# Layer 1's mixing of a two-layer diffusion block: the first map's tiles in pairs, by seven products of 256 tokens

## The chip, the cores and the metric

The kernel runs on one core of a Trainium2 chip. The core has a matrix engine (TensorE, PE in the rows; its weight loads are PEld), three elementwise engines (VectorE or DVE, ScalarE or ACT, GpSimd or POOL) and a queue that issues transfers (SyncE, SP). The metric is the device time of one execution in microseconds, the median over the runs shown.

## The reference, cut to what matters

Two layers over 512 tokens of width 1024. Every layer ends in a squared-ReLU mixing:

```
def _sq_relu_mlp(h, w1, w2):
    return jnp.square(jax.nn.relu(h @ w1)) @ w2
h_lat = h_lat + mod_l[5] * _sq_relu_mlp(
    _modulate(_rmsnorm(h_lat, norm2_g[i]), mod_l[3], mod_l[4]), mlp_w1[i], mlp_w2[i])
```

`w1` is 1024 x 4096 and `w2` is 4096 x 1024, all in float32. The change is in `h @ w1` of layer 1; after that layer only the final norm is left.

## The kernel before, in words

Everything lies with channels on the 128 partitions and the 512 tokens along a row. A float32 product is made of three products of two-part numbers: an operand is split into a high part (a cast on ACT) and a low part (the difference, on DVE or POOL), and PE adds high x high, high x low and low x high into one buffer of PSUM (`split` L161, `proj_steps` L190). So a tile of 128 outputs with an inner size of 1024 is 8 x 3 = 24 matmuls with 512 tokens each.

`mlp` runs over four blocks of 1024 hidden channels. A block has eight f tiles (from `w1`, out of the normed activations `nh`, `nl`), each followed by `f_out`: ReLU and square on ACT, the square again and the low part `gl` on DVE. Then it has eight r tiles (from `w2`, out of `gh`, `gl`), each added into the residual `h` by `h_add` on DVE. In block 0 the first four f tiles are made in two halves of 256 tokens, as the norm of the second half comes later; in block 3 the last four r tiles are made in halves too, and the final norm hangs on them.

Weights come as tiles of 128 x 1024 floats. SP loads them into two rings of buffers `raw` (four and three, tile k goes to ring k mod 2); each is then split into `whi`, `wlo` (two buffers in a ring), the cast always on ACT, the low part on DVE or POOL by turns (`w_prep`). `w_next` asks for loads seven tiles ahead and splits two ahead. Each engine takes its instructions in the order in which the program writes them, and waits on semaphores of the others. `residual` and `residual_norm` make r tiles, `grow` makes a piece of the modulation on DVE (in layer 0's mixing, 48 pieces). PSUM gives six buffers `mm` of 512 floats for f and r tiles.

Of the kernel before, what the change touches and what calls it, by code (L numbers as in the profile page):

```python
# [93 lines left out]
def body(ctx: ExitStack, tc: tile.TileContext, I, out):  # L94
# [6 lines left out]
    def f32(ap):  # L101
        return ap.bitcast(F32)
# [86 lines left out]

    def proj_steps(ps, w, ah, al, t0=0, n=T):  # L190
        k = len(ah)
        for i in range(k):
            c = slice(i * P, (i + 1) * P)
            wh = w[0]
            pe.matmul(ps, wh[:, c], ah[i][:, t0 : t0 + n], start=(i == 0), stop=False)  # L195
            yield
            pe.matmul(ps, wh[:, c], al[i][:, t0 : t0 + n], start=False, stop=False)  # L197
            yield
        for i in range(k):
            wl = w[1]  # L200
            pe.matmul(ps, wl[:, i * P : (i + 1) * P], ah[i][:, t0 : t0 + n], start=False, stop=(i == k - 1))  # L201
            yield

    def proj(*a):
        for _ in proj_steps(*a):
            pass
# [1229 lines left out]

    gk = [0]

    def grow(n=1):
        for _ in range(n):  # L1440
            k = gk[0]
            if k == len(gq):
                return
            gk[0] += 1
            while len(gin) < k + 2:
# [137 lines left out]

    def mlp(layer, ah_, al_, nrm, i_norm, shift_in, last_norm, mod_next, load=None):
        gate = mods[:, layer, 5, :]
        for blk in range(4):
            gh, gl = [None] * 8, [None] * 8
# [15 lines left out]
            def pair(f, n, mids):  # L1603
# [398 lines left out]
```

## Time and profile before

| what | value |
| --- | --- |
| median of 3 runs (lowest, highest) | 1123.25 us (1123.15, 1125.39) |
| the profiled execution, its own time | 1122.43 us |
| its span from first to last instruction | 1120.6 us |
| mean granted TensorE clock | 0.989 |
| PE, DVE, ACT, POOL busy, share of the span | 97%, 62%, 39%, 37% |

The span is shorter than the execution's time by 1.8 us, which lie around it. Shares are means over stages of different kinds: layer 0's mixing with attention and long convolution is the first third, the two mixings by `mlp` are most of the rest. "Busy" of PE counts matmuls whose ends are modelled, so the pace is read from start to start of matmuls. What an engine waits for is in the lists of waits; idle time of an engine that nobody waits for costs nothing.

### The profile page before, as it was taken

The page shows a single profiled execution, that of the slowest core. Times are in us where ns is not written, and L with a number is a line of the kernel's source. Part 1 is how long each engine was busy: PE and PEld are TensorE (multiplying, and loading weights), DVE is VectorE, ACT ScalarE, POOL GpSimd, SP SyncE. Part 2 cuts the span into 40 slices and gives each one's busy share as a digit, 9 for nine tenths or more (in the row PEclk, how much of TensorE's full clock was granted, in tenths as well). Part 3 has the DMA queues.
Part 4 walks back from the last instruction along what each step waited for, and adds up shares of the span by engine and source line. Part 5 has one row for each costly group of instructions (what it writes and reads, how often), then busy time and mean ns, then how long its engine had stood idle before and what let it go on. Part 6 is the DMA issues. An engine that isn't in the chain of part 4 may idle for free.

```text
span 1120.6 us, 14729 instructions
## 1 busy us (share of the span) xinstructions
PE 1087.8 (97%) x5740; PEld 918.4 (82%) x5740; DVE 691.4 (62%) x1026; ACT 439.2 (39%) x740; POOL 412.4 (37%) x308
## 2 busy tenths in 40 slices
PE   8899999999999999999999999899999999999996
PEld 5488988788989988888888888898888888888886
DVE  6589899989856646686686674677333323322334
ACT  4455346666554531331242233375313312411431
POOL 4457337885654423122132123265211311231112
PEclk9899999999999999999999999999999999999998
DMA  9786754225432327457557553213322332231302
GB/s 339 273 270 213 255 172 138 71 69 170 150 134 76 114 94 245 168 199 242 198 189 241 187 173 132 76 39 113 113 75 75 113 113 75 76 126 62 113 1 75
DMA packets 48650, 161.36 MB, mean 144 GB/s; under 512 B 5250, under 2 KB 8578, under 8 KB 48452
## 3 DMA queue, kind: packets, MB, share of 16 engines
q1 hardware_dynamic: 46132, 149.93, 39.2%
q0 software_dynamic: 2448, 10.49, 2.7%
q8 instruction: 45, 0.74, 0.3%
q14 instruction: 25, 0.20, 0.1%
HBM read 156.20 MB, written 4.20 MB: 143 GB/s over the span
## 4 chain that ended last, share of the span: by engine, by line
PE 80%; DVE 11%; ACT 2%; DMA 2%; issue 2%; POOL 2%; SPq 0%; POOLq 0%; DVEq 0%; ACTq 0%
PE r L195 11%; PE r L197 11%; PE r L201 11%; PE f L201 10%; PE f L197 10%; PE f L195 10%; PE v L876 2%; DVE g L627 2%; PE u L195 1%; DVE nl L1509 1%; PE u L201 1%; PE u L197 1%; DMA g<-in_adaN 1%; PE f L1610 1%; DVE mx L1053 1%
## 5 line engine op out<-in xcount | busy, mean ns | idle before, releaser
L164 POOL TENSOR_TENSOR wlo<-raw,whi 128x1024 fp32r<-128x1024 f32 x77 | 194.6, 2531 | 518.1 <-ACT whi L163 384.7
L163 ACT CAST whi<-raw 128x1024 fp32r<-128x1024 f32 x135 | 139.8, 1042 | 174.5 <-PE r L197 153.9
L195 PE MATMUL r<-gh,whi 128*128 128x512 f32 (+1 forms) x576 | 207.3, 368 | 0.0
L197 PE MATMUL r<-gl,whi 128*128 128x512 f32 (+1 forms) x576 | 207.0, 368 | 0.0
L195 PE MATMUL f<-nh,whi 128*128 128x512 f32 (+1 forms) x512 | 191.4, 379 | 0.0
L197 PE MATMUL f<-nl,whi 128*128 128x512 f32 (+1 forms) x512 | 191.3, 378 | 0.0
L1522 DVE SCALAR_TENSOR_TENSOR h<-r,mods,h 128x512 f32<-128x512 f32 (+1 forms) x81 | 54.3, 671 | 170.0 <-PE r L201 169.8
L1600 DVE TENSOR_TENSOR r<-r 128x512 f32<-128x512 f32 (+1 forms) x72 | 53.8, 748 | 159.1 <-ACT gh L1599 159.0
L1598 ACT ACTIVATE r<-f 128x512 f32<-128x512 f32 (+1 forms) x72 | 39.5, 548 | 236.7 <-PE f L201 235.1
L201 PE MATMUL r<-gh,wlo 128*128 128x512 f32 (+1 forms) x576 | 130.2, 368 | 0.0
L195 PEld LDWEIGHTS r<-gh,whi 128*128 128x128 f32 x576 | 108.3, 188 | 19.2
L197 PEld LDWEIGHTS r<-gl,whi 128*128 128x128 f32 x576 | 108.4, 188 | 19.0
L201 PE MATMUL f<-nh,wlo 128*128 128x512 f32 (+1 forms) x512 | 121.3, 379 | 0.0
L201 PEld LDWEIGHTS r<-gh,wlo 128*128 128x128 f32 x576 | 100.5, 188 | 18.9
L195 PEld LDWEIGHTS f<-nh,whi 128*128 128x128 f32 x512 | 96.2, 188 | 19.0
L197 PEld LDWEIGHTS f<-nl,whi 128*128 128x128 f32 x512 | 96.3, 188 | 18.9
L201 PEld LDWEIGHTS f<-nh,wlo 128*128 128x128 f32 x512 | 92.3, 188 | 18.9
L1451 DVE CUSTOM_DVE_ANT_0 g<-g,sbcl 128x1024 f32<-128x1024 f32 x48 | 105.2, 2191 | 0.0
L164 DVE TENSOR_TENSOR wlo<-raw,whi 128x1024 fp32r<-128x1024 f32 x58 | 75.9, 1308 | 8.4 <-ACT whi L163 8.4
L195 PE MATMUL u<-ah,whi 128*128 128x512 f32 x160 | 63.3, 395 | 0.8 <-DVE v L882 0.8
L197 PE MATMUL u<-al,whi 128*128 128x512 f32 x160 | 62.5, 391 | 0.0
L723 POOL TENSOR_TENSOR wlo<-raw,whi 128x1024 fp32r<-128x1024 f32 x17 | 42.5, 2499 | 37.3 <-ACT whi L714 35.5
(374 smaller groups left out, 1874.3 us busy)
## 6 DMA issues: line engine op xcount, KB each, us to landing
raw<-in_w SPq DMA_DIRECT2D x128, 512.0 KB, 4.4
g<-in_adaT SPq DMA_DIRECT2D x80, 512.0 KB, 4.2
g<-in_adaN SPq DMA_DIRECT2D x16, 512.0 KB, 9.0
raw<-in_w_hy SPq DMA_DIRECT2D x12, 512.0 KB, 4.3
raw<-in_w_qk SPq DMA_DIRECT2D x8, 512.0 KB, 4.0
pth<-in_pth POOLq DMA_DIRECT2D x4, 768.0 KB, 6.3
raw<-in_w_out SPq DMA_DIRECT2D x5, 512.0 KB, 4.0
x<-in_xT SPq DMA_DIRECT2D x8, 256.0 KB, 6.4
```

What stands on the lines that cost most here:

```text
L163: act.copy(out=hi, in_=src)
L164: (lo_eng or dve).tensor_tensor(out=lo, in0=src, in1=f32(hi), op=ALU.subtract)
L195: pe.matmul(ps, wh[:, c], ah[i][:, t0 : t0 + n], start=(i == 0), stop=False)
L197: pe.matmul(ps, wh[:, c], al[i][:, t0 : t0 + n], start=False, stop=False)
L201: pe.matmul(ps, wl[:, i * P : (i + 1) * P], ah[i][:, t0 : t0 + n], start=False, stop=(i == k - 1))
L627: dve.tensor_tensor_reduce(out=g, in0=g, in1=sbc[0], scale=1.0, scalar=0.0, op0=ALU.mult, op1=ALU.add, accum_out=mods[:, 0, 2 + k // ND, k ...
L723: ew(pool if k else dve).tensor_tensor(out=wts[k][1], in0=raws[k], in1=f32(wts[k][0]), op=ALU.subtract)
L876: pe.matmul(pp[:, :256], a, b, start=(k == 0 and e == 0), stop=(k == ND - 1 and e == 2))
L1451: dve.tensor_tensor_reduce(out=gin[k], in0=gin[k], in1=sbc[0], scale=1.0, scalar=0.0, op0=ALU.mult, op1=ALU.add, accum_out=mods[:, layer, ...
L1522: dve.scalar_tensor_tensor(out=hs[d][:, seg], in0=pp[:, :n], scalar=gate[:, d : d + 1], in1=hs[d][:, seg], op0=ALU.mult, op1=ALU.add)
L1598: act.activation(out=r, in_=pp[:, :n], func=AF.Relu)
L1600: dve.tensor_tensor(out=r, in0=r, in1=r, op=ALU.mult)
```

## The change

In layer 1 the f tiles of blocks 1, 2 and 3 are made two at a time (`pair7`), twelve pairs. Two tiles are a product of weights cut in 2 x 2 (two tiles, two halves of the 1024 inputs) with activations cut in 2 x 2 (two halves of the inputs, two halves of the tokens); a form of Strassen's scheme makes it by seven products and not eight. A product is 4 x 3 matmuls of 256 tokens. The seven go in this order (buffer in PSUM, weights): `px` first half, W0; `py` first, W0; `py` second, W1; `pz` second, W2; `px` second, W3; `px` first, W1; `pz` first, W2. W0 is the first tile's weights, W1, W2 and W3 are or hold sums of both tiles' weights: POOL makes one sum into the scratch tile `scr` and one in place, DVE makes two into `scr` (`pair_sums`). The sums of the activations are made once, during block 0's r tiles (`act_sums`, into `th` and over the second half of `nh`, `nl`). The seven products are put together by five adds on DVE out of PSUM (into `s1`, `s2`, named r in the rows, and `u3`, named na) and a copy on ACT (`p1`). `finish` of a pair, six activations on ACT (ReLU, square, square again for each tile) and two low parts `gl` on DVE, is written into the next pair, behind its second and third product. `late=2` puts the last two of eight steps at the end of the r tile that follows the last pair.

```
...
+    def proj_steps(ps, w, ah, al, t0=0, n=T, late=0):
...
+        for part in (range(k - late), range(k - late, k)):
+            for i in part:
...
+    def w_split(k, src, eng, n=1024):
+        pl, tg, nr, nb, rp = streams["st"[k % 2]]
+        hi = pl.tile([P, 1024], F32R, name=nm("whi"), tag=tg + "whi", bufs=nb)
+        lo = pl.tile([P, 1024], F32R, name=nm("wlo"), tag=tg + "wlo", bufs=nb)
+        split(hi[:, :n], lo[:, :n], src, eng)
+        return hi, lo
+    def pair_sums(k):
+        if k in sums_done or k not in pairs:
+            return
+        sums_done.add(k)
+        a, b, t = wraw[k], wraw[k + 1], scr[0]
+        dve.tensor_tensor(out=t[:, :T], in0=b[:, :T], in1=a[:, :T], op=ALU.add)
+        dve.tensor_tensor(out=t[:, T : 2 * T], in0=t[:, :T], in1=a[:, T:], op=ALU.add)
     def w_prep(n):
         while len(wsp) < min(n, len(wsrc)):
             k = len(wsp)
-            eng = (dve, pool)[k // 2 % 2]
-            wsp.append(wload(None, pool if k in fast else eng, "st"[k % 2], wraw[k]))
+            if k in pairs:
+                a, b, t = wraw[k], wraw[k + 1], scr[0]
+                pool.tensor_tensor(out=t[:, 2 * T : 3 * T], in0=a[:, :T], in1=b[:, :T], op=ALU.add)
+                pool.tensor_tensor(out=b[:, :T], in0=b[:, :T], in1=b[:, T:], op=ALU.add)
+                wsp.append(w_split(k, a, pool))
+            elif k - 1 in pairs:
+                pair_sums(k - 1)
+                wsp.append(w_split(k, scr[0][:, : 2 * T], dve))
+            else:
+                eng = (dve, pool)[k // 2 % 2]
+                wsp.append(wload(None, pool if k in fast else eng, "st"[k % 2], wraw[k]))
...
+            th = ml.tile([P, 4, 2, 3, 256], F32R, name=nm("th"), tag="pth")
+            scr[0] = ml.tile([P, 2048], F32, name=nm("scr"), tag="ptl")
+            pairs.update(k0 + 16 * blk + f for blk in (1, 2, 3) for f in (0, 2, 4, 6))
+        def act_sums(i):
+            b1, b2, t = (ml.tile([P, T], F32, name=nm("b"), tag="sq", bufs=3) for _ in range(3))
+            x, y = slice(0, 256), slice(256, 512)
+            pool.tensor_tensor(out=b1, in0=f32(ah_[i]), in1=f32(al_[i]), op=ALU.add)
+            pool.tensor_tensor(out=b2, in0=f32(ah_[i + 4]), in1=f32(al_[i + 4]), op=ALU.add)
+            dve.tensor_tensor(out=t[:, x], in0=b1[:, x], in1=b1[:, y], op=ALU.subtract)
+            dve.tensor_tensor(out=t[:, y], in0=b2[:, y], in1=b1[:, y], op=ALU.subtract)
+            yield
+            dve.scalar_tensor_tensor(out=b1[:, y], in0=t[:, y], scalar=-1.0, in1=b1[:, x], op0=ALU.mult, op1=ALU.subtract)
+            dve.scalar_tensor_tensor(out=b2[:, y], in0=b1[:, y], scalar=-1.0, in1=b2[:, x], op0=ALU.mult, op1=ALU.subtract)
+            split(th[:, i, 0, 0:2, :], th[:, i, 1, 0:2, :], t.rearrange("p (a t) -> p a t", a=2), pool)
+            split(th[:, i, 0, 2, :], th[:, i, 1, 2, :], b1[:, y], pool)
+            split(ah_[i][:, y], al_[i][:, y], b2[:, y], pool)
+            yield
...
+        def product(o, w, c, b):
+            for i in range(4):
+                l = w[0][:, c + i * P : c + (i + 1) * P]
+                pe.matmul(o, l, b[i][0], start=(i == 0), stop=False)
+                pe.matmul(o, l, b[i][1], start=False, stop=False)
+            for i in range(4):
+                pe.matmul(o, w[1][:, c + i * P : c + (i + 1) * P], b[i][0], start=False, stop=(i == 3))
...
+            def pair7(f, before):
+                k = wk[0]
+                wk[0] += 2
+                w_fetch(k + 7)
+                w0, w1 = wsp[k], wsp[k + 1]
+                w2 = w_split(k, wraw[k + 1], dve)
+                x, y = slice(0, 256), slice(256, 512)
+                px, py, pz = ps_m("f"), ps_m("f"), ps_m("f")
+                small = [ml.tile([P, 256], F32, name=nm("na"), tag="na", bufs=4) for _ in range(2)]
+                p1, u3 = small
+                s1 = ml.tile([P, T], F32, name=nm("r"), tag="r", bufs=3)
+                twice = lambda v: v.rearrange("p (a t) -> p a t", a=1).to_broadcast([P, 2, 256])
+                both = lambda v: v.rearrange("p (a t) -> p a t", a=2)
+                product(px[:, x], w0, 0, b_part(0, 0))
+                act.copy(out=p1, in_=px[:, x])
+                product(py[:, x], w0, T, b_part(1, 0))
+                w3 = w_split(k + 1, scr[0][:, 2 * T : 3 * T], pool, T)
+                before(0)
+                product(py[:, y], w1, 0, t_part(2))
+                dve.tensor_tensor(out=both(s1), in0=both(py), in1=twice(p1), op=ALU.add)
+                before(1)
+                w_fetch(k + 9)
+                w_prep(k + 3)
+                product(pz[:, y], w2, 0, t_part(0))
+                product(px[:, y], w3, 0, t_part(1))
+                dve.tensor_tensor(out=u3, in0=px[:, y], in1=s1[:, y], op=ALU.add)
+                dve.tensor_tensor(out=s1[:, y], in0=pz[:, y], in1=s1[:, y], op=ALU.add)
+                pair_sums(k + 2)
+                product(px[:, x], w1, T, b_part(1, 1))
+                dve.tensor_tensor(out=s1[:, y], in0=px[:, x], in1=s1[:, y], op=ALU.add)
+                w_prep(k + 4)
+                product(pz[:, x], w2, T, [(ah_[i][:, y], al_[i][:, y]) for i in range(4)])
+                s2 = ml.tile([P, T], F32, name=nm("r"), tag="r", bufs=3)
+                dve.tensor_tensor(out=both(s2), in0=both(pz), in1=twice(u3), op=ALU.add)
+                for u in range(2):
+                    mk = att_tile if f + u < 4 else w_tile
+                    gh[f + u], gl[f + u] = mk("gh"), mk("gl")
+                def finish(part):
+                    for u, s, sign in ((0, s1, 1.0), (1, s2, -1.0)):
+                        if part != 1:
+                            act.activation(out=s, in_=s, func=AF.Relu, scale=sign)
+                            act.activation(out=gh[f + u], in_=s, func=AF.Square)
+                            act.activation(out=s, in_=s, func=AF.Square)
+                        if part != 0:
+                            dve.tensor_tensor(out=gl[f + u], in0=s, in1=f32(gh[f + u]), op=ALU.subtract)
+                return finish
...
+            if blk and seven:
+                fin7 = lambda part: None
+                for f in range(0, 8, 2):
+                    fin7 = pair7(f, fin7)
+                fin7(2)
+            else:
+                for f in range(f0, 8):
...
+                    if seven and blk == 0 and d % 2 == 0:
+                        sums_ = act_sums(d // 2)
...
+                    proj(pp, w, gh, gl, late=2 if blk and seven and d == 0 else 0)
...
+                    if seven and blk == 0:
+                        next(sums_)
...
+                residual_norm(gh, gl, gate, last_norm, mod_next, hook=None, late=2 if seven else 0)
...
+    mlp(0, dh, dl, n1, 1, sh1, n2, mod_n2, pool_load, seven=False)
```

What the order shows at three places. On PE before, the 24 matmuls of a tile wait at the first for ACT and at the first of the low part, for DVE or POOL, and nowhere else. On PE after, second pair of block 1, from product 5 (weights 8118) into product 6 (weights 8061); both write the buffer 8087, which is `px` (numbers are those of the buffers):

```order
L1655 MATMUL f_1500_8087<-th_1357_7168,whi_1506_8118 128x256
L1656 MATMUL f_1500_8087<-th_1357_7168,whi_1506_8118 128x256
L1658 MATMUL f_1500_8087<-th_1357_7168,wlo_1507_8119 128x256 [waits Pool_49]
L1658 MATMUL f_1500_8087<-th_1357_7168,wlo_1507_8119 128x256 x3
L1655 MATMUL f_1500_8087<-nh_1323_7054,whi_1491_8061 128x256 [waits DVE_49]
L1656 MATMUL f_1500_8087<-nl_1331_7062,whi_1491_8061 128x256
L1655 MATMUL f_1500_8087<-nh_1324_7055,whi_1491_8061 128x256
L1656 MATMUL f_1500_8087<-nl_1332_7063,whi_1491_8061 128x256
```

Product 6 has a wait for DVE at its first matmul, though its weights were in use at product 3. On DVE, two tiles of block 1 before:

```order
L1600 TENSOR_TENSOR r_1489_8037<-r_1489_8037 128x512 [waits Activation_49]
L1601 TENSOR_TENSOR gl_1487_8011<-r_1489_8037,gh_1486_8010 128x512 [waits DVE_49]
L164 TENSOR_TENSOR wlo_1492_8045<-raw_1462_7890,whi_1491_8044 128x1024 [waits DMAHW7_49,PE_49,Activation_49]
L1600 TENSOR_TENSOR r_1496_8075<-r_1496_8075 128x512 [waits Activation_49]
L1601 TENSOR_TENSOR gl_1494_8049<-r_1496_8075,gh_1493_8048 128x512 [waits DVE_49]
```

Two passes for a tile, and a low part of weights. On DVE after, what stands in the second pair of block 1, from the low part of W2 to that of the next pair (8088 is `py`, 8087 `px`, 8089 `pz`; `gl` belongs to the pair before, `raw`, `scr` and the last `wlo` to the pair behind):

```order
L164 TENSOR_TENSOR wlo_1499_8084<-raw_1461_7833,whi_1498_8083 128x1024 [waits Activation_49]
L1715 TENSOR_TENSOR r_1505_8092<-f_1501_8088,na_1503_8090 128x512 [waits PE_49,Activation_49]
L1741 TENSOR_TENSOR gl_1495_8080<-r_1484_7967,gh_1494_8079 128x512 [waits DVE_49,Activation_49]
L1741 TENSOR_TENSOR gl_1497_8082<-r_1493_8077,gh_1496_8081 128x512 [waits DVE_49,Activation_49]
L1721 TENSOR_TENSOR na_1504_8091<-f_1500_8087,r_1505_8092 128x256 [waits DVE_49,PE_49]
L1722 TENSOR_TENSOR r_1505_8092<-f_1502_8089,r_1505_8092 128x256 [waits DVE_49]
L1430 TENSOR_TENSOR scr_1358_7169<-raw_1472_7914,raw_1465_7873 128x512 [waits DMAHW6_49,DMAHW5_49,Pool_49]
L1431 TENSOR_TENSOR scr_1358_7169<-scr_1358_7169,raw_1465_7873 128x512 [waits DVE_49]
L1725 TENSOR_TENSOR r_1505_8092<-f_1500_8087,r_1505_8092 128x256 [waits PE_49]
L164 TENSOR_TENSOR wlo_1513_8195<-scr_1358_7169,whi_1512_8194 128x1024 [waits Activation_49]
L1729 TENSOR_TENSOR r_1514_8210<-f_1502_8089,na_1504_8091 128x512 [waits PE_49]
L164 TENSOR_TENSOR wlo_1520_8217<-raw_1472_7914,whi_1519_8216 128x1024 [waits Activation_49]
```

The instruction that product 6 waits for, L1721, stands behind two `gl` that wait for ACT, and the weight sums at L1430 wait for POOL. On POOL after, at the same place (8119 is the low part of W3, then the sums and the low part of W0 of the next pair):

```order
L164 TENSOR_TENSOR wlo_1507_8119<-scr_1358_7169,whi_1506_8118 128x512 [waits PE_49,Activation_49]
L1438 TENSOR_TENSOR scr_1358_7169<-raw_1465_7873,raw_1472_7914 128x512 [waits DMAHW6_49,DMAHW5_49,Pool_49]
L1439 TENSOR_TENSOR raw_1472_7914<-raw_1472_7914 128x512 [waits Pool_49]
L164 TENSOR_TENSOR wlo_1511_8150<-raw_1465_7873,whi_1510_8149 128x1024 [waits PE_49,Activation_49]
L164 TENSOR_TENSOR wlo_1528_8252<-scr_1358_7169,whi_1527_8251 128x512 [waits DVE_49,PE_49,Activation_49]
```

Before, POOL had there only low parts of weights, two for every four tiles; now it has four instructions in every pair.

## Rows read from the trace of the kernel before

**Rows 1.** The page's head: busy us, share of the span and instructions.

```profile
span 1120.6 us, 14729 instructions
...
PE 1087.8 (97%) x5740; PEld 918.4 (82%) x5740; DVE 691.4 (62%) x1026; ACT 439.2 (39%) x740; POOL 412.4 (37%) x308
```

**Rows 2.** Stretches of layer 1's mixing: busy us by engine, granted clock, DMA.

```profile
800.00:850.00 50.00, 50.00 (x218) 40.75 (x218) 14.74 (x15) 10.70 (x12) 10.03 (x4) 1.00 0.31 105
...
1000.00:1050.00 50.00, 50.00 (x218) 40.75 (x218) 15.53 (x19) 14.01 (x18) 8.18 (x5) 1.00 0.31 104
```

**Rows 3.** Waits in 782:1064: us in total, times, longest.

```profile
POOL wlo L164 <- ACT whi L163: 134.8, 13, 21.9
ACT r L1598 <- PE f L201: 114.0, 27, 11.9
DVE r L1600 <- ACT gh L1599: 100.1, 27, 5.0
DVE h L1522 <- PE r L201: 90.0, 24, 4.8
```

**Rows 4.** Timeline of PE: first matmul of tiles; start us, us.

```profile
1041.91 0.39 PE L195 MATMUL f<-nh,whi 128*128 128x512 f32 x1
...
1086.10 0.28 PE L195 MATMUL r<-gh,whi 128*128 128x256 f32 x1
...
1094.64 0.28 PE L195 MATMUL r<-gh,whi 128*128 128x256 f32 x1
```

**Rows 5.** Groups by form, PE: busy us, mean ns of one, idle before.

```profile
L195 PE MATMUL r<-gh,whi 128*128 128x256 f32 x64 | 15.7, 283 | 0.0
...
L195 PEld LDWEIGHTS r<-gh,whi 128*128 128x128 f32 x193 | 36.2, 188 | 8.2
```

**Rows 6.** Timelines of PE and DVE where one waits for the other.

```profile
808.11 1.98 PE L201 MATMUL r<-gh,wlo 128*128 128x512 f32 x8
...
810.13 0.75 DVE L1522 SCALAR_TENSOR_TENSOR h<-r,mods,h 128x512 f32<-128x512 f32 x1 [4.70 <-PE r L201]
...
732.65 0.68 DVE L1740 TENSOR_TENSOR zl<-z,zh 128x512 fp32r<-128x512 f32 x1
...
733.48 0.36 PE L1729 MATMUL z<-whi,nh 128*128 128x256 f32 x1 [0.16 <-DVE zl L1740]
```

**Rows 7.** Groups by form of DVE, ACT, POOL; one low part in DVE's timeline.

```profile
816.39 1.22 DVE L164 TENSOR_TENSOR wlo<-raw,whi 128x1024 fp32r<-128x1024 f32 x1
...
L1601 DVE TENSOR_TENSOR gl<-r,gh 128x512 fp32r<-128x512 f32 x28 | 19.4, 692 | 1.0
L1740 DVE TENSOR_TENSOR zl<-z,zh 128x512 fp32r<-128x512 f32 x8 | 5.0, 680 | 0.2
L1311 DVE TENSOR_TENSOR yo<-yq,y 128x256 f32<-128x256 f32 x4 | 1.7, 415 | 0.0
...
L163 ACT CAST whi<-raw 128x1024 fp32r<-128x1024 f32 x69 | 71.5, 1042 | 85.9 <-PE r L197 80.4 <-PE f L197 3.7 <-issue 1.9
L1599 ACT ACTIVATE gh<-r 128x512 fp32r<-128x512 f32 x28 | 17.7, 632 | 0.9
L1819 ACT COPY nbs<-nb 128x256 f32<-128x256 f32 x1 | 0.4, 372 | 1.2 <-PE nb L221 1.2
...
L1325 POOL TENSOR_TENSOR hyl<-yo,hyh 128x512 fp32r<-128x512 f32 x3 | 3.9, 1288 | 4.2 <-ACT hyh L1320 4.2
L164 POOL TENSOR_TENSOR nl<-na,nh 128x256 fp32r<-128x256 f32 x9 | 6.7, 746 | 9.3 <-ACT nh L163 8.7 <-PE f L195 0.5
```

**Rows 8.** Timelines of POOL and DVE, both operands in SBUF.

```profile
821.27 2.39 POOL L164 TENSOR_TENSOR wlo<-raw,whi 128x1024 fp32r<-128x1024 f32 x1 [13.72 <-PE r L201]
821.85 2.90 DVE L164 TENSOR_TENSOR wlo<-raw,whi 128x1024 fp32r<-128x1024 f32 x1
...
850.89 0.69 DVE L1601 TENSOR_TENSOR gl<-r,gh 128x512 fp32r<-128x512 f32 x1
851.15 2.69 POOL L164 TENSOR_TENSOR wlo<-raw,whi 128x1024 fp32r<-128x1024 f32 x1 [21.88 <-ACT whi L163]
```

**Rows 9.** Timelines of DVE and POOL, DVE reading z in PSUM.

```profile
732.65 3.67 DVE L1740 TENSOR_TENSOR zl<-z,zh 128x512 fp32r<-128x512 f32 x6
733.11 2.41 POOL L164 TENSOR_TENSOR wlo<-raw,whi 128x1024 fp32r<-128x1024 f32 x1 [1.06 <-ACT whi L163]
```

**Rows 10.** Stretches around two stops of PE (columns as in Rows 2).

```profile
204.00:206.10 2.10, 0.03 (x2) 0.02 (x1) 2.10 (x6) 0.99 (x2) 2.04 (x2) 1.00 0.62 224
206.10:210.00 3.90, 3.76 (x26) 3.38 (x26) 3.76 (x4) 1.65 (x4) 3.61 (x5) 1.00 0.03 14
719.80:724.70 4.90, 1.99 (x17) 1.73 (x16) 4.34 (x7) 1.76 (x4) 2.28 (x2) 1.00 0.29 120
724.70:728.10 3.40, 3.40 (x19) 3.40 (x18) 1.28 (x4) 1.35 (x3) 0.43 (x1) 0.50 0.02 5
```

**Rows 11.** DMA issues on the page: count, KB each, us to landing.

```profile
raw<-in_w SPq DMA_DIRECT2D x128, 512.0 KB, 4.4
```

More of the change, by code (lines that the diff above doesn't have):

```diff
@@ L188, in mm3, with proj @@
         pe.matmul(ps, ll, rh, start=False, stop=last)
-    def proj_steps(ps, w, ah, al, t0=0, n=T):
+    def proj_steps(ps, w, ah, al, t0=0, n=T, late=0):
         k = len(ah)
[L192 to L205, printed above, removed]
+        for part in (range(k - late), range(k - late, k)):
+            for i in part:
+                c = slice(i * P, (i + 1) * P)
+                wh = w[0]
+                pe.matmul(ps, wh[:, c], ah[i][:, t0 : t0 + n], start=(i == 0), stop=False)
+                yield
+                pe.matmul(ps, wh[:, c], al[i][:, t0 : t0 + n], start=False, stop=False)
+                yield
+            for i in part:
+                wl = w[1]
+                pe.matmul(ps, wl[:, i * P : (i + 1) * P], ah[i][:, t0 : t0 + n], start=False, stop=(i == k - 1))
+                yield
+    def proj(*a, late=0):
+        for _ in proj_steps(*a, late=late):
             pass
@@ L1407, in w_fetch @@
             wraw.append(ahead.pop(3 + k) if k < 3 else wfetch(wsrc[k], "st"[k % 2]))
+    pairs, sums_done, scr = set(), set(), [None]
+    def w_split(k, src, eng, n=1024):
[11 more added lines that the diff above has]
+        dve.tensor_tensor(out=t[:, T : 2 * T], in0=t[:, :T], in1=a[:, T:], op=ALU.add)
     def w_prep(n):
@@ L1435, in g_fetch @@
             gin.append(g)
-    gk = [0]
+    gk, glim = [0], [len(gq)]
     def grow(n=1):
@@ L1441, in grow @@
             k = gk[0]
-            if k == len(gq):
+            if k == glim[0]:
                 return
             gk[0] += 1
-            while len(gin) < k + 2:
+            while len(gin) < min(k + 2, glim[0]):
                 n0 = len(gin)
@@ L1536, in residual, with residual_norm @@
             grow()
-    def residual_norm(kh, kl, gate, nrm, mod_a, d0=0):
+    def residual_norm(kh, kl, gate, nrm, mod_a, d0=0, hook=None, late=0):
         fin = []
@@ L1544, in residual_norm @@
             pp = ps_m("r")
-            proj(pp, w, kh, kl)
+            proj(pp, w, kh, kl, late=late if d == d0 else 0)
             h_add(d, 0, T, pp, gate)
+            if hook and d == d0 + 1:
+                hook()
             while fin:
@@ L1582, in w_more, with mlp, b_part, t_part @@
         w_prep(len(wsp) + 1)
-    def mlp(layer, ah_, al_, nrm, i_norm, shift_in, last_norm, mod_next, load=None):
+    def mlp(layer, ah_, al_, nrm, i_norm, shift_in, last_norm, mod_next, load=None, seven=True):
         gate = mods[:, layer, 5, :]
+        k0 = wk[0]
+        th = None
+        if seven:
+            th = ml.tile([P, 4, 2, 3, 256], F32R, name=nm("th"), tag="pth")
[8 more added lines that the diff above has]
+            dve.tensor_tensor(out=t[:, y], in0=b2[:, y], in1=b1[:, y], op=ALU.subtract)
+            yield
+            dve.scalar_tensor_tensor(out=b1[:, y], in0=t[:, y], scalar=-1.0, in1=b1[:, x], op0=ALU.mult, op1=ALU.subtract)
[3 more added lines that the diff above has]
+            split(ah_[i][:, y], al_[i][:, y], b2[:, y], pool)
+            yield
+        def b_part(half, t):
+            seg = slice(t * 256, (t + 1) * 256)
+            return [(ah_[half * 4 + i][:, seg], al_[half * 4 + i][:, seg]) for i in range(4)]
+        def t_part(n):
+            return [(th[:, i, 0, n, :], th[:, i, 1, n, :]) for i in range(4)]
+        def product(o, w, c, b):
[5 more added lines that the diff above has]
+                pe.matmul(o, w[1][:, c + i * P : c + (i + 1) * P], b[i][0], start=False, stop=(i == 3))
         for blk in range(4):
```

16 lines of the change are left out of this document (6 added, 10 removed).

## The prediction

> **What bounds the kernel now.** The page comes first: TensorE (PE) is busy for 97% of the span, the next engine, DVE, for 62% [rows 1]. A share over the whole span says little about layer 1, so next come the stretches: in layer 1's mixing PE is busy 50.00 us of every 50, at a granted clock of 1.00 (2.4 GHz), while DVE works some 15 of 50 and POOL 8 to 10 [rows 2]. The list of waits over 782:1064 has not one line in which PE waits; the others wait for PE, or for each other with PE running on [rows 3]. So the stretch is paced by PE alone, and its pace is in PE's timeline. From 1041.91 to 1086.10 PE makes eight tiles of 24 matmuls with 512 tokens: 44.19/192 = 0.230 us each. From 1086.10 to 1094.64 it makes three times 24 with 256 tokens: 8.54/72 = 0.1186 each, a weight load with every one [rows 4]. Half the tokens cost 0.515 of the time, so halving by itself loses 3%, not more.
>
> **PE's own sum.** Before, a pair of tiles is 48 matmuls of 512 tokens: 48 x 0.230 = 11.05 us. After, it is seven products of 12 matmuls with 256 tokens: 84 x 0.1186 = 9.96, or 1.42 a product. That is 1.08 less; three blocks of four pairs make 12: **-13.0 us**, if PE never waits.
>
> **The wait in front of the sixth product.** By the order, product 6 waits for a DVE instruction, and that one is `u3`: it reads the other half of the same buffer `px`, into which product 5 has just been made. Product 6 can't start before product 5 has ended, been read, and DVE has told PE. The last matmul of product 5 ends 0.28 after its start [rows 5]; DVE starts 0.04 later (the eight matmuls at 808.11 end at 810.09, the add starts at 810.13 [rows 6]); a DVE add of 256 with one operand from PSUM takes 0.415 [rows 7]; PE resumes 0.15 after DVE's end (DVE 732.65 + 0.68 = 733.33, PE at 733.48 [rows 6]). Sum 0.885, less the 0.12 that a matmul takes anyway: 0.76 a pair, twelve times **+9.2**. It can't be less, since nothing is queued between the two products on PE. The Trainium skill ("PSUM — Partial Sum Buffer", PSUM bank collisions raise a hardware error) says to guard PSUM by bank and not by address: by that the wait is needed and its 9.2 us stand, by addresses alone the two halves would be free of each other and the 9.2 would fall away. No row of before shows two halves of a bank in use at once.
>
> **Elementwise work, and who can do it at once.** Before, a pair needs two casts and two low parts of weights, and eight passes over tiles. After, for each pair: on POOL two sums and a low part of 512 at 1.29 and a low part of 1024 at 2.39 [rows 7, 8], 6.3 us; on DVE two low parts of 1024 at 1.22, two weight sums and two `gl` of 512 at 0.69 [rows 7], 5.2, and five adds out of PSUM, 0.68 x 2 + 0.415 x 3 = 2.6; on ACT three casts of 1.04, one of 0.63, a copy of 0.37 and six activations of 0.63 [rows 7], 7.9. Each engine stays below 9.96. But POOL and DVE aren't free of each other. DVE's low part at 821.85 takes 2.90, not 1.22: POOL began its own at 821.27 and held until 823.66, and DVE ends 1.09 behind that. The other way round, POOL's low part at 851.15 takes 2.69 and not 2.39, as DVE's `gl` of 850.89 runs to 851.58: it ends 2.26 behind that [rows 8]. Whoever comes second is stopped, and gets back 0.13. Out of PSUM it isn't so: DVE's `zl`, one operand in PSUM, passes POOL's 2.41 at 0.61 to 0.68 each [rows 9]. The Trainium skill ("SBUF — State Buffer", SBUF: two separate sides) calls it an exclusive lock for the whole instruction, on a DVE instruction with two SBUF inputs and one of GpSimd, and the other fully blocks; the trace agrees but for the 0.13. By the page alone, with nothing given back, the sum below would be +16 and not +10.
>
> So POOL's 6.3 and DVE's 5.2 with two SBUF operands go one behind the other: 11.5 us, less 0.13 for each of some six hand-overs: 10.7. A pair with the wait above alone is 9.96 + 0.76 = 10.72. The pair of engines is full to the last, and every moment in which neither can go lengthens something.
>
> **A pair, queue by queue.** I laid out the four queues in the order of the program with these durations: an engine starts its next instruction when it is free and what it waits for is done, two-operand DVE work and POOL work never together. For the third pair of block 1, from its first matmul:
> - The weight sums on DVE ask 0.07 after POOL has begun its low part of 2.39, and are stopped until that is done; the second sum ends at 1.46. ACT's cast of W1 runs 1.49 to 2.53, W2 to 3.48, the copy to 3.77, W3 to 4.31, and only then come the six activations of the tiles of the pair before, up to 8.06.
> - DVE: low part of W1 until 3.79, of W2 4.32 to 5.54 (product 3 and 4 wait 0.14 and 0.33 for them), the add behind product 3 until 6.15. Then `gl` twice, which needs ACT: the first is stopped by POOL's low part of W3 and ends at 7.25, the second asks at 8.10, is stopped by POOL's sum and ends at 8.95.
> - `u3` stands behind that second `gl` on DVE. Product 5 ends at 7.75; `u3` runs 8.87 to 9.29, and product 6 starts at 9.44 where 0.76 would have made it 8.35: 1.09 more.
>
> The pair is 9.96 + 0.14 + 0.33 + 1.85 = 12.28. The same way for blocks 2 and 3, where what differs is how late the second `gl` ends: the first pair has no finished tiles in front, 9.96 + 0.76 = 10.72; the second waits 1.80 at product 6, 11.76; the third 1.08, 11.04; the fourth 1.69 there and 0.47 at products 3 and 4, 12.12: a block of 45.6 us where it was 44.2, so +1.4 each. In block 1 the sums of activations come on top: POOL and DVE make them during the eight r tiles before (four times two sums of 512, a low part of 512 and two of 256 at 0.75 on POOL [rows 7], 5.4 us; on DVE four of 256), the last quarter is behind the last h-add, and product 3 of the first pair needs it: it waits some 3.2 us, its pair is 14.3, and the queues start the second pair late (12.7, then 12.3 and 12.1). That block is 51.5, +7.3.
>
> **Edits at nothing.** The sums of activations of the first three quarters lie under two r tiles of PE each, 11 us for 5.4 on POOL; without that cover each would cost what the fourth does. `late` moves the first use of the last pair's second tile in the r tile behind it from 14 x 0.23 = 3.2 us to 20 x 0.23 = 4.6; its high part is there about 2.0 us after product 7 (add 0.72, two activations 1.27) and its low part at 3.3, needed at 4.8 and not 3.4, so it's hidden either way, by 0.1 without `late`. SP loads the same tiles in the same order; a raw buffer's last reader is now the low part of W2, and what is loaded into it is used by the sums two pairs later, some 24 us, where a load lands in 4.4 [rows 11]. `grow` has nothing left to do in layer 1.
>
> **The sum.** -13.0 + 9.2 + what the port and the queues add (2.7 in block 2, 2.7 in block 3, 8.6 in block 1) = +10.2. The profiled execution took 1122.43 us; with +10.2 it is 1132.6. The median of the runs is 0.8 higher, so **1133.4, forecast 1133 us**, 0.9% slower. What a measurement of this kernel can tell from no change is 0.2%, 2.2 us.
>
> **Rivals.**
> 1. *The collisions fall elsewhere* (ends faster). With POOL and DVE passing each other without loss, and the last quarter ready in time, -13.0 + 9.2 = -3.8: 1119.4. It decides at one point: whether the second `gl` is done before product 5 ends, in every pair; ACT would have to be done by 7.0 instead of 8.06. For it: each engine has room alone. Against it: 11.5 us of port work in 10.7. Chance 0.12.
> 2. *Half of them do*: within 0.2%, 1121 to 1125.5. The 0.13 handed back might be 0.3, which takes the sum from +10 to +4, and so does 10% less on DVE or POOL; two of them reach zero. Chance 0.13.
> 3. *Every pair is as slow as the steady one, or slower*: without any hand-back a steady pair comes to 13.06, and the sum to +16; 10% more on ACT adds 4, on POOL 7. 1137 to 1143. Chance 0.22.
> 4. *The clock falls.* In 719.80:724.70 PE stood for 2.51 and 0.40 and ran thin matmuls, and the granted clock was then 0.50 (1.2 GHz) for 3.40 us; after 2.07 us of standing at 204 to 206 between dense matmuls it stayed at 1.00 [rows 10]. Waits of 1.85 in dense work are nearer to the second. A fall takes 3.40 us of work at half pace, 1.7 us; once (first pair of block 1) it is in my range, at each of some eight long waits it would be +14, 1147. Chance 0.13.
> 5. *The products don't save PE time*, if matmuls of 256 were paced by their weight loads: a load's row says 188 ns [rows 5], and 84 x 0.188 would be 15.8 a pair, +57 in all, 1180. But the 72 matmuls of [rows 4] have their loads as well and go at 0.1186. Chance 0.02.
>
> My own case, 1127 to 1137, has the rest, 0.38. Faster by over 0.2%: 0.12. Within: 0.13. Slower: 0.75. The range from 1121 to 1147 leaves out rival 1 mostly and the end of 4 and 5.
>
> **What would show it.** PE matmuls of 256 at 0.119 from start to start within a product; a stop of PE before product 6 in every pair, near 0.8 in the first pair of blocks 2 and 3 and near 1.9 in the others, with DVE `na` (L1721) named as releaser; DVE sums at L1430 of 2.9 and `gl` of 0.8 to 1.0, POOL sums of 1.6; a stop of some 3 us at product 3 in block 1's first pair, behind the cast of `th`. I am wrong if L1741 and L1430 run at 0.69, if PE waits under 1 us a pair, or if the clock row shows 0.50 between 840 and 1070.

## The result and the profile after

The changed kernel takes 1134.25 us (median of 4 runs, 1131.07 to 1135.20) where the kernel before took 1123.20 beside it: 1.0091 times as long, 95% interval 1.0066 to 1.0117. The page's head of after:

```profile
span 1132.8 us, 15916 instructions
...
PE 1083.6 (96%) x6172; PEld 934.0 (82%) x6172; DVE 769.3 (68%) x1114; ACT 480.3 (42%) x812; POOL 492.3 (43%) x364
```

PE's busy time is 4.2 us less than in [rows 1] and the span is 12.2 longer: PE now waits. (That busy time also counts the modelled end of a matmul before every stop, and a stretch at half clock, so the 4.2 isn't what the seven products save; that is read below from pairs without a wait.) Stretches of after (most of block 1's pairs, then mainly its r tiles, then mainly block 2's pairs; columns as in [rows 2]):

```profile
843.00:888.00 45.00, 38.66 (x294) 36.75 (x292) 34.26 (x39) 22.14 (x34) 26.83 (x17) 0.96 0.23 78
888.00:932.00 44.00, 42.58 (x209) 35.58 (x209) 18.11 (x21) 16.69 (x22) 17.89 (x8) 1.00 0.32 113
932.00:976.00 44.00, 40.98 (x308) 38.85 (x307) 29.82 (x34) 19.14 (x28) 22.11 (x12) 1.00 0.20 72
```

The waits of after in 782:1085 (us in total, times, longest); [rows 3] had no line of PE:

```profile
PE f L1655 <- DVE na L1721: 13.9, 12, 1.6
...
PE f L1655 <- ACT th L163: 2.2, 1, 2.2
...
PE f L1656 <- POOL th L164: 0.4, 1, 0.4
```

`na` at L1721 is `u3`: twelve pairs, twelve stops before product 6. The list counts from the modelled end of the matmul before; from start to start, less the 0.12 that a matmul takes, the twelve are 15.8 us, and stops named in the text below are in that measure. PE's timeline at the first matmul of a block's first pair and at the first r matmul behind its last:

```profile
844.67 0.28 PE L1655 MATMUL f<-nh,whi 128*128 128x256 f32 x1
...
896.18 0.39 PE L197 MATMUL r<-gh,whi 128*128 128x512 f32 x1
...
940.37 0.28 PE L1655 MATMUL f<-nh,whi 128*128 128x256 f32 x1
...
986.07 0.39 PE L197 MATMUL r<-gh,whi 128*128 128x512 f32 x1
...
1030.26 0.28 PE L1655 MATMUL f<-nh,whi 128*128 128x256 f32 x1
...
1075.97 0.39 PE L197 MATMUL r<-gh,whi 128*128 128x512 f32 x1
```

The three blocks take 51.51, 45.70 and 45.71, together 142.92, where three of 44.19 [rows 4] are 132.57: **+10.35**. This sum over the twelve pairs is the measure used below, since stretches that the change doesn't touch differ by some us from one execution to the next (block 1 starts at 844.67 here and started at 843.07 before, ahead of any pair). It ends at the first r matmul, so a stop inside the r tile behind a block isn't in it.

### The profile page after: what moved, and what is told of

It is laid out like the page before. It is cut to its first block, busy times and chain, and to the rows that moved or that the text cites. A ratio compares the mean times of both kernels' runs of the same rounds, so it can differ in the third digit from the quotient of the medians.

```text
span 1132.8 us, 15916 instructions
## 1 busy us (share of the span) xinstructions
PE 1083.6 (96%) x6172; PEld 934.0 (82%) x6172; DVE 769.3 (68%) x1114; ACT 480.3 (42%) x812; POOL 492.3 (43%) x364
## 4 chain that ended last, share of the span: by engine, by line
PE 71%; DVE 14%; ACT 4%; issue 4%; DMA 3%; POOL 3%; SPq 0%; POOLq 0%; ACTq 0%; DVEq 0%
PE r L197 11%; PE r L199 10%; PE r L203 10%; PE f L199 6%; PE f L203 6%; PE f L197 6%; DVE g L629 3%; PE f L1655 2%; PE f L1658 2%; PE f L1656 2%; DMA g<-in_adaN 1%; DMA g<-in_adaT 1%; DVE nl L1542 1%; DVE scr L1430 1%; ACT whi L163 1%
## 5 line engine op out<-in xcount | busy, mean ns | idle before, releaser
L164 POOL TENSOR_TENSOR wlo<-raw,whi 128x1024 fp32r<-128x1024 f32 x77 | 191.5, 2489 | 360.0 <-ACT whi L163 305.4
L197 PE MATMUL f<-nh,whi 128*128 128x512 f32 (+1 forms) x320 | 116.0, 370 | 0.0
L199 PE MATMUL f<-nl,whi 128*128 128x512 f32 (+1 forms) x320 | 116.0, 370 | 0.0
L1673 DVE TENSOR_TENSOR r<-r 128x512 f32<-128x512 f32 (+1 forms) x48 | 37.6, 784 | 67.9 <-ACT gh L1672 67.8
L164 DVE TENSOR_TENSOR wlo<-raw,whi 128x1024 fp32r<-128x1024 f32 x58 | 75.0, 1294 | 12.2 <-ACT whi L163 12.2
L1671 ACT ACTIVATE r<-f 128x512 f32<-128x512 f32 (+1 forms) x48 | 25.1, 523 | 131.6 <-PE f L203 130.0
L203 PE MATMUL f<-nh,wlo 128*128 128x512 f32 (+1 forms) x320 | 73.1, 371 | 0.0
L199 PEld LDWEIGHTS f<-nl,whi 128*128 128x128 f32 x320 | 60.2, 188 | 10.8
L197 PEld LDWEIGHTS f<-nh,whi 128*128 128x128 f32 x320 | 60.2, 188 | 10.8
L203 PEld LDWEIGHTS f<-nh,wlo 128*128 128x128 f32 x320 | 56.3, 188 | 10.8
L1655 PE MATMUL f<-nh,whi 128*128 128x256 f32 x192 | 48.9, 287 | 13.9 <-DVE na L1721 13.9
```

The costliest lines, as they stand in the source:

```text
L164: (lo_eng or dve).tensor_tensor(out=lo, in0=src, in1=f32(hi), op=ALU.subtract)
L1655: pe.matmul(o, l, b[i][0], start=(i == 0), stop=False)
L1671: act.activation(out=r, in_=pp[:, :n], func=AF.Relu)
L1673: dve.tensor_tensor(out=r, in0=r, in1=r, op=ALU.mult)
```

## The experiments

e1 to e11 were timed in five rounds beside the kernel before (medians 1123.97, 1125.47 and 1124.92 in the three sets). "Pairs" is the sum just explained, worked out from the same rows of each run's timeline.

| run | median | ratio (95%) | pairs |
| --- | --- | --- | --- |
| before | | 1 | 132.57 |
| changed kernel | 1134.25 | 1.0091 (1.0066-1.0117) | 142.92 |
| e1 u3 first | 1136.80 | 1.0111 (1.0091-1.0131) | 142.83 |
| e2 own bank | 1130.48 | 1.0057 (1.0037-1.0078) | 139.92 |
| e3 W0's low part on DVE | 1139.14 | 1.0146 (1.0123-1.0169) | 148.47 |
| e4 early sums | 1129.69 | 1.0057 (1.0035-1.0078) | 139.29 |
| e5 as e3, behind u3 | 1125.34 | 1.0007 (0.9993-1.0021) | 134.22 |
| e6 reordered | 1123.49 | 0.9982 (0.9964-1.0001) | 129.98 |
| e7 reordered, own bank | 1112.69 | 0.9888 (0.9864-0.9911) | 120.38 |
| e8 as e7, sums behind product 5 | 1126.55 | 1.0008 (0.9994-1.0021) | 132.26 |
| e9 all in order | 1115.58 | 0.9920 (0.9904-0.9936) | 122.97 |
| e10 as e9, W0's low part on POOL | 1124.04 | 0.9996 (0.9980-1.0011) | 133.15 |
| e11 as e9, shared bank | 1120.13 | 0.9965 (0.9948-0.9982) | 129.58 |

**One part at a time: e1 to e4.**

e1 moves `before(1)`, the two `gl` of the pair before, from behind product 3 to behind `u3`:

```
                 dve.tensor_tensor(out=s1[:, y], in0=pz[:, y], in1=s1[:, y], op=ALU.add)
+                before(1)
```

e2 gives product 6 a buffer `pw` of its own, e3 puts W0's low part on DVE, e4 makes both halves of the first quarter of `act_sums` in the first r tile and the rest one tile earlier:

```
-                product(px[:, x], w1, T, b_part(1, 1))
+                product(pw[:, x], w1, T, b_part(1, 1))
...
-                wsp.append(w_split(k, a, pool))
+                wsp.append(w_split(k, a, dve))
...
-                    if seven and blk == 0 and d % 2 == 0:
+                    if seven and blk == 0 and d in (0, 1, 3, 5):
```

e1: 

> Of the changed kernel alone: u3 and the add behind it now stand ahead of the two gl of the pair before on DVE. Queue theory (the stop before product 6 is 0.76 for the read of the other half, and what is above 0.76 is DVE's queue; that work does not vanish but is late elsewhere): the stops before product 6 all fall to 0.76, 7.7 us less in sum, but the gl now push the weight sums and with them the cast and low part of W1 back, so that product 3 of the third and fourth pairs waits 1.1 for its cast and some 0.4 and 0.3 for low parts, and the r tile behind a block waits 1.2 for the last gl; worked out queue by queue the kernel is 3 us longer, 1137. Rival, a local wait: only u3's place counts, nothing else gets late, 7.7 us shorter, 1126.5.

e2: 

> Product 6 goes into a fourth PSUM buffer of its own (pw) instead of the first half of px, so nothing of product 5 has to be read first; nothing else differs from the changed kernel. Queue theory: all twelve stops before product 6 go, but product 7 writes the other half of pz, which DVE reads (s1 of L1722) right behind u3, so where u3 is late PE stops there instead, 0.7 to 0.9 in steady pairs and 0.2 in second ones, and with PE ahead products 1, 3 and 4 wait 0.25 to 0.46 more for casts and low parts: 3 us shorter, 1131. Rival, the half of the bank is all of it: the 15.6 us of stops before product 6 go, 1118.6.

e3: 

> The low part of W0 (1024 elements) is made by DVE instead of POOL: 1.22 instead of 2.39 a pair, so the work that POOL and DVE can't do at once falls from 11.5 to 10.3 us a pair, while DVE's own queue grows by 1.22. Port theory: 2 us shorter, 1132, with the weight sums of L1430 back from 2.9 to 0.7 in steady pairs. Rival, DVE's queue alone counts (no exclusion): DVE has 1.2 more in front of u3 or of the low part of W1, and the kernel is 5 to 10 us longer, 1139 to 1144.

e4: 

> The sums of activations start one r tile earlier in block 0 (both halves of the first quarter in the first r tile, then one half a tile), so the last quarter is done one r tile before block 1; nothing else differs. Queue theory: the stops of 2.18 and 0.42 at product 3 of block 1's first pair go, and with them the stretch at the low clock, so that pair comes from 15.33 to about 11, and the kernel is 3.5 to 4 us shorter, 1130.5. Rival: the stop is not from the last quarter's place but from POOL and DVE being full in that block, then the stop comes back in the second or third pair and the time stays at 1134 +- 1.

e1 gains nothing, as the queues said: its pairs are the changed kernel's, its r tiles stop on top, and the intervals of the two medians overlap; the 7.7 us less of the local wait didn't come. PE's waits in it:

```profile
PE f L1655 <- DVE na L1720: 6.2, 12, 0.5
PE f L1655 <- ACT whi L163: 3.5, 4, 0.9
PE r L199 <- DVE gl L1741: 2.3, 3, 0.8
PE f L1655 <- ACT th L163: 2.2, 1, 2.2
```

All twelve stops before product 6 are down to the least, and the time is given back in two new lines: the cast of W1, whose sums now stand behind the `gl`, and the last `gl` at the r tile behind each block. e2 took away the whole wait for `na` and gained only 3.0 us in the pairs: product 7 waits for the read of `pz` instead, and casts and low parts are late for products 1, 3 and 4. Its longest line:

```profile
PE f L1655 <- DVE r L1722: 3.7, 7, 0.6
```

e4 gave what was expected, 10.77 for block 1's first pair; the second took 12.71 where the changed kernel's took 11.79, so 0.9 of the gain came back there, as its rival said of all of it.

e3 missed by 7 us, to the rival's side. The sums at L1430 did what the port theory says (a DVE instruction with both operands in SBUF and one of POOL's aren't done at once; the second is stopped until the first ends). By-form rows of after, then of e3 (busy us, mean ns):

```profile
L1430 DVE TENSOR_TENSOR scr<-raw,raw 128x512 f32<-128x512 f32 x12 | 23.3, 1946 | 1.5 <-POOL raw L1439 1.5
```

```profile
L1430 DVE TENSOR_TENSOR scr<-raw,raw 128x512 f32<-128x512 f32 x12 | 8.2, 682 | 1.7 <-POOL raw L1439 1.7
```

But W0's low part now stood on DVE behind the second `gl` and ahead of `u3`, and six stops before product 6 grew to 1.96 to 3.61. DVE in e3's third pair of block 1:

```profile
882.78 1.27 DVE L1741 TENSOR_TENSOR gl<-r,gh 128x512 fp32r<-128x512 f32 x1 [0.43 <-ACT r L1739]
883.98 1.21 DVE L164 TENSOR_TENSOR wlo<-raw,whi 128x1024 fp32r<-128x1024 f32 x1
```

`u3` starts behind it, at 885.11. The low part didn't wait for its cast, though e5's expectation below says so: ACT ended the cast at 883.68, DVE the `gl` at 884.05. What delays `u3` is the low part's own 1.21 on top of the `gl`, and in the second pair of block 1 it took 2.19, stopped by POOL's sum. Stretches of e3: three of these stops, and what came behind each (columns as above; third from the end is the granted clock):

```profile
868.47:872.07 3.60, 0.15 (x2) 0.00 (x1) 3.47 (x4) 0.99 (x2) 2.05 (x2) 1.00 0.00 0
873.23:876.41 3.18, 3.18 (x17) 3.18 (x16) 2.22 (x3) 1.61 (x2) 0.00 (x0) 0.50 0.31 93
883.60:885.57 1.97, 0.16 (x2) 0.00 (x0) 1.94 (x4) 0.09 (x1) 0.00 (x0) 1.00 0.00 0
886.87:890.04 3.17, 3.17 (x17) 3.17 (x16) 2.08 (x3) 1.83 (x2) 0.00 (x0) 0.50 0.33 79
1055.54:1057.70 2.16, 0.16 (x2) 0.00 (x0) 2.12 (x4) 0.08 (x1) 0.09 (x1) 1.00 0.00 0
1057.70:1060.60 2.90, 2.90 (x24) 2.90 (x25) 2.12 (x4) 1.06 (x2) 0.00 (x0) 1.00 0.05 16
```

Behind five of the six the granted clock was 0.50 (1.2 GHz) for 3.4 us each (the stretches above lie within that), and products 6 and 7 of those pairs took 4.3 to 4.5 together instead of 2.96: 7.0 us in sum, more than the whole 5.55 by which e3's pairs exceed the changed kernel's. Neither of my theories had that in it.

**Is DVE too full, or was it the place: e5.** The same low part on DVE, W0's issue moved behind `u3` (`w_prep(k + 3)` behind the weight sums that follow L1722). In e5, e6 and e7 DVE's weight sums of the next pair stand ahead of POOL's sum in place and so add the tile as it was loaded, without that wait. These three therefore don't compute the layer's product and stand here for their times alone; the amount of work is the same.

> As the run with the low part of W0 on DVE, but the next pair's W0 (its POOL sums, cast and low part) is issued behind u3 and the add after it, no longer ahead of them, and W2's low part of the pair behind its first two issues. Theory: that run lost because DVE's low part of W0 stood ahead of u3 and waited for a cast that ACT makes behind its six activations, so that stops of 2 to 3.6 us arose and the clock fell behind most of them; the work that POOL and DVE can't share fell as foreseen. Then all twelve stops before product 6 are 0.76, no clock falls behind them, a steady pair is 9.96 + 0.76 + 0.23 = 10.95, and the kernel takes 1124.5. Rival: DVE is simply too full with 1.22 more a pair, wherever it stands: 1135 or more.

1125.34: the place. Eleven pairs take 10.71 to 10.95, and no clock falls behind their stops. The first pair of block 1, where e5 keeps the late sums of activations, takes 14.36.

**The bank and the port, with the queues out of the way: e6 to e8.** The edit of e6 in `pair7`, beside e4's (the split of W2 stays in its place, and W3's comes ahead of product 1, where the text on record says behind); e7 is e6 with product 6 in `pw`; e8 is e7 with `pair_sums` back at its old place, and it computes what the changed kernel does.

```
                 w2 = w_split(k, wraw[k + 1], dve)
+                w3 = w_split(k + 1, scr[0][:, 2 * T : 3 * T], dve, T)
...
                 product(py[:, x], w0, T, b_part(1, 0))
-                w3 = w_split(k + 1, scr[0][:, 2 * T : 3 * T], pool, T)
+                pair_sums(k + 2)
...
-                before(1)
...
-                pair_sums(k + 2)
...
                 w_prep(k + 4)
+                before(1)
```

e6: 

> The changed kernel with the same seven products and the same wait before product 6, but: the activation sums one r tile earlier; W2's and W3's split behind product 1, W3's low part on DVE (0.69) instead of POOL (1.29); the weight sums of the next pair behind product 2, where POOL is idle; the two gl of the pair before at the end of the pair. Queue and port theory: every extra over 0.76 before product 6 goes but in block 1's first pair (2.1), a pair is 10.72, and the kernel takes 1122.5, level with the kernel before. Rival: the extras come back in other places as they did when u3 alone was put first: 1130 to 1137.

e7: 

> As the reordered kernel, and product 6 in a fourth buffer. Theory: what is left there is the wait for the other half of px, 0.76 a pair and 2.1 once; without it a pair is 9.96 and the kernel takes 1113, 10 us below the kernel before, 9.4 below the reordered one. Rival (the wait only moves to product 7, as in the run with a buffer of its own alone, or PE is limited by something else there): 1118 to 1123.

e8: 

> As the reordered kernel with a fourth buffer, but the two weight sums of the next pair are back behind product 5 on DVE, where POOL is in its low part of W0; W3's low part is on DVE, behind product 1, still. Port theory: the first sum runs 2 to 2.9 us again instead of 0.69, the casts of W1 and all behind it are late, products 3 to 5 wait 0.4, 0.4 and 1.5 in the later pairs, and the kernel takes 13 us more than with the sums behind product 2: 1126. Rival (no exclusion; only the number of instructions on an engine counts, which is the same): within 2 us of that kernel.

All three came within 1 us of the forecast. In e6 eleven of the twelve pairs take 10.71, in e7 eleven take 9.92 to 9.94. PE's waits in e6 and then in e7:

```profile
PE f L1655 <- DVE na L1721: 7.6, 12, 1.9
```

```profile
PE f L1655 <- DVE r L1722: 0.9, 1, 0.9
```

e7 runs into product 6 at the pace of any other matmul (943.29 begins the four of product 5's low part, 943.75 product 6):

```profile
943.29 0.63 PE L1658 MATMUL f<-th,wlo 128*128 128x256 f32 x4
943.75 0.28 PE L1655 MATMUL f<-nh,whi 128*128 128x256 f32 x1
943.87 0.28 PE L1656 MATMUL f<-nl,whi 128*128 128x256 f32 x1
```

From e7 to e8 only the place of two DVE adds changes (and with it that they wait for POOL's sum), and it costs 13.9 us by the medians. Their first in e7 and in e8, by form:

```profile
L1430 DVE TENSOR_TENSOR scr<-raw,raw 128x512 f32<-128x512 f32 x11 | 7.5, 682 | 0.0
```

```profile
L1430 DVE TENSOR_TENSOR scr<-raw,raw 128x512 f32<-128x512 f32 x12 | 20.2, 1685 | 1.3 <-POOL raw L1439 1.3
```

(In e7 the first of the twelve lies ahead of the stretch shown, 843:1070.) Their wait for POOL's sum is 1.3 us in all; the add itself runs 1.00 longer in the mean, stopped. That it is the stop and not the later place is seen within e8: in blocks 2 and 3 the place is the same in every pair, and the pair whose sum ran at 0.68 (the second) takes 9.93, those whose sum took 2.06 and 2.86 (the third and the fourth) 11.15 to 11.17 and 12.29 to 12.31.

**A version with the arithmetic whole: e9 to e11.** e9 has e4's edit, the fourth buffer, W3's split ahead of product 1 (its low part on POOL), W0's low part on DVE behind `u3`, and DVE's sums behind POOL's two (`wsums`), as in the changed kernel. e10 and e11 each take one of these back: W0's low part to POOL, product 6 to `px`.

```
                 w2 = w_split(k, wraw[k + 1], dve)
+                w3 = w_split(k + 1, scr[0][:, 2 * T : 3 * T], pool, T)
...
                 product(py[:, x], w0, T, b_part(1, 0))
-                w3 = w_split(k + 1, scr[0][:, 2 * T : 3 * T], pool, T)
                 before(0)
+                wsums(k + 2)
...
                 before(1)
-                w_fetch(k + 9)
-                w_prep(k + 3)
...
                 pair_sums(k + 2)
+                w_fetch(k + 9)
+                w_prep(k + 3)
-                product(px[:, x], w1, T, b_part(1, 1))
+                product(pw[:, x], w1, T, b_part(1, 1))
```

e9: 

> A version with the changed kernel's arithmetic whole: the activation sums one r tile earlier; product 6 in a fourth buffer; W2's and W3's splits ahead of product 1's successors; W0's low part on DVE and the next pair's W0 issued behind u3; the weight sums after POOL's, as in the changed kernel. Queue and port theory: stops of 0.4 and 0.5 before product 7 in two pairs of a block, 0.1 elsewhere, and 1114.5, 20 us below the changed kernel and 9 below the kernel before. Rival: in the reordered runs the weight sums didn't wait for POOL's sum, and with that wait back the stops come back: 1120 or more.

e10: 

> As the version in order, with one word changed: W0's low part on POOL (2.39) and not on DVE (1.22). DVE has less to do and POOL has room (6.3 of 10). Port theory: DVE's two-operand work stands behind POOL's 2.39 each time, so that W2's or W3's low part is late by 1.1 and s1 by 0.4 to 0.9, 10 us more than the version in order, 1124.5. Rival without exclusion: no difference, 1114 to 1115.

e11: 

> As the version in order, but product 6 is again in the first half of px. The wait for the other half is then 0.76 to 0.87 before each product 6, and the stops before product 7 go: 6.6 us more than the version in order, 1121. Rival: hidden, since u3 is now early: no difference, 1114.5.

e9 is 0.8% faster than the kernel before (0.64% to 0.96%). e10 costs 8.5 us for one word, though it gives DVE less to do. Timeline of POOL, then of DVE, in e10:

```profile
965.52 2.82 POOL L164 TENSOR_TENSOR wlo<-raw,whi 128x1024 fp32r<-128x1024 f32 x1
```

```profile
966.82 2.07 DVE L1430 TENSOR_TENSOR scr<-raw,raw 128x512 f32<-128x512 f32 x1
968.92 0.69 DVE L1431 TENSOR_TENSOR scr<-scr,raw 128x512 f32<-128x512 f32 x1
```

and DVE at the same place in e9, where POOL has nothing left to do then:

```profile
955.57 0.68 DVE L1430 TENSOR_TENSOR scr<-raw,raw 128x512 f32<-128x512 f32 x1
956.29 0.69 DVE L1431 TENSOR_TENSOR scr<-scr,raw 128x512 f32<-128x512 f32 x1
```

POOL holds until 968.34, the add ends at 968.89, 0.55 behind: 0.14 handed back. PE's waits in e9 and then in e10 name only DVE: in e10 a low part that is late behind that add, and the read at L1730. W0's own low part on POOL isn't in the list, so its being slower there isn't the cause:

```profile
PE f L1664 <- DVE r L1730: 1.8, 6, 0.4
```

```profile
PE f L1667 <- DVE wlo L164: 7.3, 8, 1.0
PE f L1664 <- DVE r L1730: 3.0, 6, 0.6
```

e11 costs 4.6 us by the medians and 6.6 by the pairs, as foreseen by the latter.

## Why the prediction was right

**PE's own sum, -13.0.** Right: a pair without waits takes 9.92 to 9.94 in e7 (forecast 9.96) and took 11.05 before; twelve times 1.12 is 13.4. Rival 5 is out by the same rows.

**The wait before product 6, 0.76 a pair.** Right: in the first pairs of blocks 2 and 3 of after (10.71 each), and in e6, where nothing else is left, 10.71 against 9.93 in e7, so 0.78. The shared buffer costs 9.6 us there by the pairs (forecast 9.2). The Trainium skill ("PSUM — Partial Sum Buffer", PSUM bank collisions raise a hardware error) would have the wait guarded by bank, as this one is; no run here wrote one half of a bank while the other was read, so what would happen then stays open, but a second buffer makes the question idle.

**The port.** Right: e7 against e8 and e9 against e10 move work without adding an instruction, and pay 13.9 and 8.5 us. The Trainium skill ("SBUF — State Buffer", SBUF: two separate sides) has the other engine fully blocked; the rows agree but for the 0.13 to 0.14 that come back in them.

**Queue by queue.** Pairs measured, forecast in brackets: blocks 2 and 3 10.71 (10.72), 11.81 (11.76), 11.08 and 11.11 (11.04), 12.11 and 12.09 (12.12); block 1 15.33 (14.3), 11.79 (12.7), 12.30 (12.3), 12.09 (12.1), its sum 51.51 (51.5). DVE, ACT and POOL in the third pair of block 1 (it begins at 871.79):

```profile
878.00 1.07 DVE L1741 TENSOR_TENSOR gl<-r,gh 128x512 fp32r<-128x512 f32 x1
879.84 0.91 DVE L1741 TENSOR_TENSOR gl<-r,gh 128x512 fp32r<-128x512 f32 x1 [0.77 <-ACT r L1739]
880.68 0.41 DVE L1721 TENSOR_TENSOR na<-f,r 128x256 f32<-128x256 f32 x1
```

```profile
879.18 0.63 ACT L1739 ACTIVATE r<-r 128x512 f32<-128x512 f32 x1
```

```profile
878.60 1.61 POOL L1438 TENSOR_TENSOR scr<-raw,raw 128x512 f32<-128x512 f32 x1
880.28 1.61 POOL L1439 TENSOR_TENSOR raw<-raw 128x512 f32<-128x512 f32 x1
```

ACT ends its sixth activation 8.02 into the pair (forecast 8.06), the second `gl` is stopped by POOL's sum and ends at 8.96 (8.95), and `u3` runs behind it from 8.89 (8.87; a row on DVE starts some 0.07 before the row ahead of it ends). The sums at L1430, forecast at 2.9, took 0.68 to 2.88, 1.95 in the mean; `gl` (0.92 in the median) and POOL's sums at L1438 (1.61) came as forecast. So the reason was the forecast one, and e1 adds that `u3`'s place alone isn't the cure.

**Edits at nothing.** Right for the kernel as it is: PE's list has three lines, and none at the r tiles, at a load or at the first three quarters' sums. But "hidden either way" is not borne out for `late`, which no run takes away. The last `gl` of block 1:

```profile
899.26 0.69 DVE L1741 TENSOR_TENSOR gl<-r,gh 128x512 fp32r<-128x512 f32 x1 [1.16 <-ACT r L1739]
```

It ends 3.77 behind the r tile's start at 896.18 (forecast 3.3); without `late` it would be needed at 15 x 0.23 = 3.45, by the tile's sixteenth matmul. By that estimate PE would stop for 0.3 to 0.5 a block without `late`.

**What was off.** In block 1's first pair product 3 stops for 2.34 and 0.69, as forecast in sum (3.2), and the clock falls behind it: it is 0.50 from 851.15 to 854.55, of which the second line shows the middle.

```profile
848.37:850.71 2.34, 0.16 (x3) 0.00 (x1) 2.22 (x4) 0.41 (x1) 1.51 (x1) 1.00 0.98 397
851.89:854.45 2.56, 2.56 (x13) 2.56 (x13) 1.83 (x2) 1.99 (x4) 1.70 (x2) 0.50 0.00 0
```

I had that as a risk of 1.7 us, "once, in my range", and outside the sum; a 0.50 between 840 and 1070 was also on my list of signs of being wrong, and it came. Products 3 and 4 took 7.44 instead of 2.84, 4.60 more, of which the stops are 3.03: the low clock cost some 1.6. The pair is 1.0 over the forecast, and the second pair 0.9 under it, as the elementwise engines went on meanwhile (in e4, where the first is on time, it took 12.71). So that block 1's sum came out at 51.51 against 51.5 is partly luck: two misses cancel. Rival 4 was otherwise wrong for this kernel: its seven stops of 1.5 to 1.8 left the clock at 1.00, while e3 shows that a little more can make it true. Rival 2's doubt, that the 0.13 handed back might be 0.3, is settled by e10's 0.14. Rival 1's point, the second `gl` done before product 5 ends in every pair, isn't met even in e9: in its third pair of block 2 the `gl` ends at 954.87, 0.9 behind product 5. The buffer of its own keeps product 6 clear of that, and product 7 pays 0.4 to 0.5 in two pairs of a block. The rest of the 11.05 between the medians, 0.7 over the pairs, is less than what executions differ by in stretches that the change doesn't touch (1.6 ahead of block 1 in these two).

## What to carry to other kernels

Fewer operations on the busiest engine bring time only if what feeds it is early enough: here 13 us were there to be had, and e9 gets 9.3 of them by moving instructions and taking one more buffer, without one operation less than the changed kernel. Before adding work to GpSimd, sum what it and VectorE do with both operands in SBUF; an instruction moved to the faster of the two can shorten both queues, even when that one is the fuller. A wait taken away alone says little (e1, e2): look which queue is late next.

## What the runs showed of the hardware that wasn't expected

A stop of TensorE in dense work can cost more than itself. In after and e4 no stop before product 6, up to 1.78 us, was followed by a lower clock; of e3's six from 1.96 to 3.61 five were, for 3.4 us at 1.2 GHz each, and the one of 2.16 at 1055.54 was not, nor was e6's of 2.05. Nor is the length of a stop alone the measure: at product 3 of block 1's first pair e3 and e5 have the same two stops, 1.22 and 0.69 one behind the other, and the clock fell behind them in e5 (0.50 from 853.90 to 857.30) and not in e3. [Rows 10] alone (2.07 without a fall) would have said that such stops are safe. What tells the falling ones from the others stays open.
